# A two-block transformer on one core: contraction groups of 1, 2, 1, 4, 4, 4 tiles over 32 first tiles, squares on two engines, a root on ScalarE, a higher rate of the later modulation

## The chip, the core and the metric

The kernel runs on 1 core of a Trainium2 chip. The metric is the device time of one execution in microseconds. Three runs of the kernel before gave 2420.8, 2422.34 and 2423.11 us; the median is 2422.34. A further execution was recorded by the profiler.

The engines have short names in what follows: TensorE (PE, its weight loads PEld), VectorE (DVE), ScalarE (ACT), GpSimd (POOL) and SyncE (SP, whose queue issues nearly all transfers).

## The reference, cut to what matters

Sequence length 256, model width 2048, batch 1, all in float32. The part that the change touches is the head of the first block:

```python
mod = (c @ w_ada + b_ada)                      # 2048 -> 6 x 2048: shift1, scale1, gate1, ...
h = rmsnorm(x, g_pre_mix) * (1.0 + scale1) + shift1
proj = h @ w_in                                # 2048 -> q_a, k_a, v_a, q_h, f_h, i_h, g_h, gates
...                                            # attention; hgrn2 recurrence; gates; w_out; FFN
```

Behind it come the window attention, the hgrn2 recurrence (two groups of four heads), the gates, the projections, the feed-forward part, and a second block of two layers (attention and gated linear attention). They are the same in both kernels.

## The kernel before

**Tiles and chunks.** Activations lie transposed: 16 tiles of 128 of the 2048 features by 256 positions. A product in float32 is made of three matmuls: activations and weights are split into a high part (`hh`, `wh`) and the rest (`hl`, `wl`), and `mm3` issues wh x hh, wh x hl and wl x hh. Weights come in pieces of 128 x 1024 (512 KB) through a ring of five buffers (`dma_chunks`); SP's transfers use eight semaphores in turn, so that each waits for the landing of the one eight places ahead of it; ScalarE copies the high part (`split_hi`), VectorE subtracts it (`split_lo`), each into a ring of three. One piece feeds 24 matmuls of 256 columns into PSUM tiles `acc`. In this text such a piece with its 24 matmuls is a chunk.

**First stage.** `w_in` has 74 column tiles. The first `G1` = 28 of them are computed group by group along the contraction, since `h` needs the modulation (shift1, scale1), and this needs 2 x 8 MB of `w_ada`, which arrive tile by tile. `KG` says how many of the 16 contraction tiles make a group: 2, 2, 2, 2, 4, 4. In a group of g tiles a chunk holds 8/g column tiles; a group runs over all first tiles (28 x g / 8 chunks), and the partial sums are gathered in SBUF: the first group copies them there on ScalarE, the later groups add them on VectorE, two tiles (512 columns) at a time.

**Modulation pieces.** The first two thirds of the modulation come in 64 pieces of 512 KB (`_mod_flow`, `ada_load`, `ada_use`). `KP` says how many tiles of each group go over TensorE: 4 pieces a tile, as matmuls `ada` that write blocks of 32 columns; four blocks (`nq`) for groups of 2 or more, two for a group of 1. The other tiles (2 each in the last two groups) go over VectorE as a multiply with a sum (`later_piece`, tile `araw`). A list `due` says how many pieces must be used by which chunk; between those points they are spread evenly, three in a burst where possible (`BURST`). Two chunks before a group ends (`LAG`) its successor's columns are transposed (`adat`) and `first_h` is run (`hf` on VectorE, `hh` on ScalarE); at the group's end `first_lo` makes `hl` on VectorE. The first group's pieces are loaded ahead of every weight, and its tiles are the first that TensorE can use. The norm's sum of squares is made by 16 squares on ScalarE and 16 matmuls with a tile of ones (`st`), its root by shifts and three Newton steps on VectorE (`rsqrt`, L541).

**Behind the first stage.** The other tiles of `w_in` are run one by one over the whole contraction (`run`, `win`: two chunks each): the remaining rope tiles, one value tile, 28 gate tiles, 8 tiles `gh`, 4 gate tiles; then `proj` (matmuls `yp`). After each chunk `bg_step` moves background work on: the recurrence `hgrn(0)` and `hgrn(1)` one after the other, the attention `attend1` (four pairs of heads), ropes, and the later modulation (96 multiplies of 512 KB pieces on VectorE, `st_["rate"]` of them per step: `RATES[0]` in this stage, 0.7). A planner (`Clock`, `Timed`) with fixed costs decides when the next step of a background item is put into the program; the engines then execute their instructions in that order. `settle(cond)` puts in background steps without any chunk between them until a condition holds: before gate tile 12 that the first recurrence is done (`0 in ohs`, L1346), before gate tile 20 that the four attentions are, before each tile `gh` that both recurrences are (L1351).

**The recurrence's end** (L1014 to L1055): matmuls `hgx`, a copy on ScalarE (`key`), matmuls `oh`, two copies and a square on ScalarE (`P`, `R`), matmuls `hgq` (sums), twelve small steps on VectorE (`hv`, `hw`, `hr`), transposes `rbk`, a copy (`rc`), four matmuls `hrb`. **The attention's end**: exponentials `s`, scalings of `s`, transposes `atp`, copies `pt`, matmuls `ao`.

Of the kernel before, what the change touches and what calls it, by code (L numbers as in the profile page):

```python
# [7 lines left out]
F32 = mybir.dt.float32  # L8
# [3 lines left out]
AF = mybir.ActivationFunctionType  # L12
ALU = mybir.AluOpType
# [3 lines left out]
D = 2048  # L17
S = 256
META = 16
T2 = S + META  # L20
KT = D // 128
HID = 5632
FGROUPS = [16, 16, 12]
CW = 1024
KG = [2, 2, 2, 2, 4, 4]
KP = [2, 2, 2, 2, 2, 2]
BURST = 3
G1 = 28
GF = 6
G2 = 6  # L30
TF = S + 2
# [37 lines left out]
LIMITS3 = (4.0, 3.5, 1.0)  # L69
LIMITS4 = (4.0, 3.0, 1.0)  # L70
HOP = dict(pe=0.2, dve=0.1, act=0.3)
RATES = (0.7, 0.55, 0.85, 0.2)
FORCE = 2.0


# [9 lines left out]

_FCOLS = {}
_n = 0
for _name, _w in [("ident", 128), ("ones", 128), ("perm1", 128), ("cos2", T2),
                  ("sin2", T2), ("invf", 1), ("esel", 15), ("lo1", 1), ("lo2", 1)]:
    _FCOLS[_name] = (_n, _w)  # L90
    _n += _w
# [4 lines left out]
def _tile_chunks(ap, nk):  # L96
    kc = nk if nk <= 8 else nk // 2
    return [ap[:, k0 * 128:(k0 + kc) * 128] for k0 in range(0, nk, kc)]


def _mod_flow():


    flow, j0 = [], 0
    for g, p in zip(KG, KP):
        pe = [("pe", j0, p, i) for i in range(4 * p)]
# [9 lines left out]
def _plan(a):  # L116

    plan = [a["w_first"][i] for i in range(a["w_first"].shape[0])]
    for i in range(74 - G1):
        plan += _tile_chunks(a["w_in"][i], KT)  # L120
# [99 lines left out]
def body(ctx, tc, a, out, dbg=None):  # L220
# [3 lines left out]
    cst = ctx.enter_context(tc.tile_pool(name="cst", bufs=1))  # L224
# [19 lines left out]
    def bank(name):  # L244
        return ps.tile([128, 512], F32, tag="b", name=name)
# [24 lines left out]
    def t1(name="t1", T=S, dt=F32):  # L270
        return t1p.tile([128, T2], dt, tag="t", name=name)[:, :T]
# [5 lines left out]
    def small(name, n):  # L277
# [3 lines left out]
    TE = Timed(nc.tensor, clock, "pe", lambda n, kw: n / 2400.0 * (  # L281
        4.0 if "lhsT" in kw and kw["lhsT"].dtype == F32 else 1.0) + 0.0025 if n > 16 else 0.11)
    VE = Timed(nc.vector, clock, "dve", lambda n, kw: max(0.07 + n / 960.0, 0.13))
# [3 lines left out]
    tt = VE.tensor_tensor  # L287
    stt = VE.scalar_tensor_tensor
    ts = VE.tensor_scalar
    act = SE.activation  # L290
# [12 lines left out]
    x, xs = [], []  # L303
# [14 lines left out]
    def C(name, i=0, n=None):  # L318
        o, w = _FCOLS[name]
        n = w - i if n is None else n  # L320
        return fc[:, o + i:o + i + n]

    ident = C("ident")
    ones = C("ones")
    identr = cst.tile([128, 128], F32R, name="identr")
    maskr = cst.tile([128, 2 * 128], F32R, name="maskr")
    hh = [cst.tile([128, T2], F32R, name=f"hh{k}") for k in range(KT)]
# [5 lines left out]
    eps1 = cst.tile([128, 1], F32, name="eps1")  # L333
    spare1 = cst.tile([128, 1], F32, name="spare1")
    VE.memset(eps1, 1e-6)


    plan = _plan(a)
# [6 lines left out]
    def dma_chunks(upto):  # L345
        while ptr["dma"] < min(upto, len(plan)):
            i = ptr["dma"]
            n = plan[i].shape[1]
            raws[i] = raw_tile("raw")
            SY.dma_start(out=raws[i][:, :n], in_=plan[i])  # L350
            ptr["dma"] += 1
# [183 lines left out]
    def newton(v, r, t):  # L535

        stt(out=t, in0=r, scalar=-0.5, in1=v, op0=ALU.mult, op1=ALU.mult)
        tt(out=t, in0=t, in1=r, op=ALU.mult)
        stt(out=r, in0=t, scalar=1.5, in1=r, op0=ALU.add, op1=ALU.mult)

    def rsqrt(v, r, t):  # L541

        ts(out=t.bitcast(I32), in0=v.bitcast(I32), scalar1=1, scalar2=None,
           op0=ALU.arith_shift_right)
        ts(out=r.bitcast(I32), in0=t.bitcast(I32), scalar1=-1, scalar2=0x5F3759DF,
           op0=ALU.mult, op1=ALU.add)
        for _ in range(3):
            newton(v, r, t)
# [248 lines left out]
    R = slice(META, T2)  # L797
# [381 lines left out]


    st = bank("st")
    for k in range(KT):
        sq = t1()
        act(out=sq, in_=x[k][:, R], func=AF.Square)
        TE.matmul(st[:, :S], lhsT=ones, rhs=sq, start=(k == 0), stop=(k == KT - 1))
    rbs, v, w = t1("rbs"), t1("rv"), t1("rw")
    ts(out=v, in0=st[:, :S], scalar1=1.0 / D, scalar2=1e-6, op0=ALU.mult, op1=ALU.add)
    rsqrt(v, rbs, w)

    flow = _mod_flow()  # L1190
    ada_todo += [x for f in flow for x in f]
# [7 lines left out]
    def first_lo(k):  # L1199
        stt(out=hl[k][:, :S], in0=hfs.pop(k), scalar=modv(0, k), in1=hh[k][:, :S].bitcast(F32),  # L1200
            op0=ALU.add, op1=ALU.subtract)
# [17 lines left out]
    dma_chunks(4)  # L1219
    for k in range(KG[0]):  # L1220
        first_h(k)
    split_lo(1)
    for k in range(KG[0]):
        first_lo(k)

    ends = [G1 * sum(KG[:i + 1]) // 8 - LAG for i in range(len(KG) - 1)]
    due = [(e, sum(len(f) for f in flow[:i + 2])) for i, e in enumerate(ends)]
    used, want, at, fins = n0, float(n0), 0, []
    k0 = 0
    for gi, g in enumerate(KG):  # L1230
        m = 8 // g
        nch = G1 // m
        last = gi == len(KG) - 1
        for c in range(nch):
            wh, wl = next_chunk()
            banks = []
            if at == 0:

                banks = [bank("acc") for _ in range(m // 2)]
                for w_, h_ in ((wh, hh), (wl, hh), (wh, hl)):  # L1240
                    for i in range(m):
                        for kk in range(g):
                            TE.matmul(banks[i // 2][:, i % 2 * S:(i % 2 + 1) * S],
                                      lhsT=w_[:, (i * g + kk) * 128:(i * g + kk + 1) * 128],
                                      rhs=h_[kk][:, :S],
                                      start=h_ is hh and w_ is wh and kk == 0 and i % 2 == 0,
                                      stop=h_ is hl and kk == g - 1, skip_group_check=True)
# [19 lines left out]
            for i, p in enumerate(banks):  # L1267
                dst, then = first_place(c * m + i * 2)
                p = p.rearrange("p (a t) -> p a t", a=2)
                if gi == 0:  # L1270
                    SE.copy(dst, p)
                else:
                    tt(out=dst, in0=p, in1=dst, op=ALU.add)
                if last:
                    spawn(then, "first")
# [30 lines left out]
        k0 += g  # L1306
    st_["rate"] = RATES[0]
    spawn(hgrn(1), "hg")

    for n in range(G1 - 24, 9):  # L1310
        win(evac_rope1, n)
# [43 lines left out]
    finish("hg", "att", "rope")  # L1355
    st_["rate"] = RATES[1]
    for n in range(KT):
# [106 lines left out]
    finish("pair")  # L1464
    st_["rate"] = RATES[2]
    y, yacc = tiles("y", KT, S), [t1("yacc"), t1("yacc")]
# [65 lines left out]
    for gi, gn in enumerate(FGROUPS):  # L1532
        zz["h"], zz["l"] = tiles("zh", gn, S, F32R), tiles("zl", gn, S, F32R)
        n0 = 0
        if gi == 0:
            next_layer(y, yacc, S, None, S, lambda k: gcol[:, 2, k:k + 1], GF, TF, evac_ff)
            dump("x1", x[5])
            later_sets(5)
            st_["rate"] = RATES[3]
            n0 = GF  # L1540
# [508 lines left out]
    def gla_gate(n, g):  # L2049
# [11 lines left out]
                  v=(evac_gv, False), g=(evac_go, True))  # L2061
# [32 lines left out]
    for k in range(0, KT, 2):  # L2094
# [6 lines left out]
        else:  # L2101
# [3 lines left out]
                          in_=o)  # L2105
# [29 lines left out]
def _layout(inp):  # L2135
    import numpy as np
    f = {k: np.asarray(v) for k, v in inp.items()}
    a = {}
# [6 lines left out]
    for p in sum(_mod_flow(), []):  # L2145
        if p[0] == "pe":
            _, j0, g, i = p
# [4 lines left out]
        else:  # L2152
# [4 lines left out]
    w = f["w_in"][0]  # L2157
# [6 lines left out]
             + g_h + gab[28:])  # L2164
    first = _pack(np, w, order[:G1])
    parts, k0 = [], 0
    for g in KG:
        m = 8 // g
        parts.append(first[:, :, k0 * 128:(k0 + g) * 128].reshape(
            G1 // m, m, 128, g * 128).transpose(0, 2, 1, 3).reshape(G1 // m, 128, CW))  # L2170
        k0 += g
# [13 lines left out]
    start = dict(q=0, k=2048, v=3072, g=4096)  # L2185
# [4 lines left out]
    start = dict(q=(0, 256), k=(1024, 256), v=(2048, 512), g=(4096, 512))  # L2190
# [18 lines left out]
    f32 = np.float32  # L2209
    p = np.arange(128)  # L2210
    perm1 = np.zeros((128, 128), f32)
# [9 lines left out]
    t = np.arange(S)  # L2221
    angs = np.zeros((128, T2), f32)
    for pp in range(128):
# [4 lines left out]
    esel[:, 7] = 1.0  # L2228
    neg = -f32(2.0) ** 126
    sidx, tidx = p[:, None], p[None, :]  # L2230
    fcs = dict(ident=np.eye(128, dtype=f32), ones=np.ones((128, 128), f32), perm1=perm1,
               cos2=np.cos(angs.astype(np.float64)).astype(f32),
               sin2=(np.sin(angs.astype(np.float64)) * turn).astype(f32),
               invf=invf, esel=esel, lo1=np.where(p % 64 // 16 == 1, f32(-1), f32(0))[:, None],
# [30 lines left out]
```

## Time and profile before

| what | kernel before |
|---|---|
| median of 3 runs | 2422.34 us |
| the profiled execution | 2425.35 us |
| its span, first to last instruction | 2423.4 us |
| TensorE busy | 2391.2 us, 99% |
| VectorE busy | 1724.0 us, 71% |
| ScalarE busy | 1195.8 us, 49% |
| read from HBM | 492.68 MB, 204 GB/s over the span |
| mean granted TensorE clock | 0.994 |

The profiled execution is 3.0 us longer than the median, and 2 us of it lie outside the span. Busy time on TensorE is pipelined time: an engine that shows 10.00 of 10 us may still run its matmuls at the lower clock, so the granted clock of a stretch stands beside it. An idle engine costs time where the last-ending chain goes through it; here that is TensorE for 94% of the span.

### The profile page before, as it was taken

What the parts mean: (1) busy time and instruction counts of PE and PEld (TensorE: products, weight loads), DVE (VectorE), ACT (ScalarE), POOL (GpSimd) and SP (SyncE); (2) the same over time, 40 slices, a digit from 0 to 9 for tenths busy, and PEclk for the clock granted to TensorE, in tenths of its full rate; (3) what the DMA queues carried; (4) which work ended last, traced back from release to release, by engine and by line L of the source; (5) the groups of instructions that cost most, each with busy time, mean ns of one, the idle gap of its engine ahead of it and who ended that gap; (6) DMA issues with size and microseconds to landing.
All of it is one profiled execution on the core that took longest, in us unless ns stands there. A gap on an engine that the chain in (4) does not pass through costs nothing.

```text
span 2423.4 us, 49168 instructions
## 1 busy us (share of the span) xinstructions
PE 2391.2 (99%) x20217; PEld 2349.9 (97%) x20217; DVE 1724.0 (71%) x2986; ACT 1195.8 (49%) x1923; POOL 63.3 (3%) x128
## 2 busy tenths in 40 slices
PE   8999999999999999999999999999999999999998
PEld 7999999999999999999999999999999999999997
DVE  4897978888867775577755666777777466788664
ACT  4335565444445444444434444545555456855443
POOL 0000000000000000000000000121110000000000
PEclk9999999999999999999999999999999999999999
DMA  9975768798885666666665556554443545444453
GB/s 400 364 288 171 235 201 267 247 307 295 305 291 161 210 223 223 221 218 220 225 211 186 184 170 170 173 162 140 151 145 118 174 149 173 160 137 147 158 183 113
DMA packets 144273, 501.33 MB, mean 207 GB/s; under 512 B 17088, under 2 KB 19904, under 8 KB 144048
## 3 DMA queue, kind: packets, MB, share of 16 engines
q1 hardware_dynamic: 139840, 493.15, 60.6%
q0 software_dynamic: 3072, 3.35, 0.4%
q8 instruction: 158, 2.59, 0.4%
q10 hardware_dynamic: 1136, 1.68, 0.2%
q14 instruction: 67, 0.55, 0.1%
HBM read 492.68 MB, written 2.10 MB: 204 GB/s over the span
## 4 chain that ended last, share of the span: by engine, by line
PE 94%; DMA 3%; DVE 2%; ACT 1%; issue 0%; SPq 0%; DVEq 0%; ACTq 0%
PE acc L214 76%; PE wave L214 5%; PE yp L214 4%; PE hgs L214 1%; DMA araw<-in_w_adat 1%; PE sc L214 1%; DVE wl L214 1%; PE go L214 1%; PE st L214 1%; PE ada L214 1%; PE o L214 1%; DMA araw<-in_w_mod 1%; DMA raw<-in_w_out 1%; PE tp L214 0%; DVE araw L214 0%
## 5 line engine op out<-in xcount | busy, mean ns | idle before, releaser
L214 ACT CAST wh<-raw 128x1024 fp32r<-128x1024 f32 (+1 forms) x754 | 774.2, 1027 | 1100.8 <-PE acc L214 710.2
L214 PE MATMUL acc<-hh,wh 128*128 128x256 f32 (+2 forms) x4112 | 1182.3, 288 | 2.5 <-ACT hh L214 2.5
L214 PE MATMUL acc<-hl,wh 128*128 128x256 f32 (+2 forms) x4112 | 1165.2, 284 | 3.7 <-DVE hl L214 3.7
L214 PE MATMUL acc<-hh,wl 128*128 128x256 f32 (+2 forms) x4112 | 1166.3, 284 | 2.3 <-DVE wl L214 2.3
L214 DVE TENSOR_TENSOR wl<-raw,wh 128x1024 fp32r<-128x1024 f32 (+1 forms) x754 | 900.1, 1194 | 369.5 <-ACT wh L214 365.8
L214 PEld LDWEIGHTS acc<-hh,wh 128*128 128x128 f32 x4112 | 778.5, 189 | 10.9 <-issue 5.2
L214 PEld LDWEIGHTS acc<-hl,wh 128*128 128x128 f32 x4112 | 778.2, 189 | 5.3 <-DVE hl L214 4.3
L214 PEld LDWEIGHTS acc<-hh,wl 128*128 128x128 f32 x4112 | 778.4, 190 | 3.3 <-DVE wl L214 3.1
L214 PE MATMUL acc<-zl,wh 128*128 128x256 f32 x704 | 198.2, 282 | 0.0
L214 PE MATMUL acc<-zh,wl 128*128 128x256 f32 x704 | 198.0, 281 | 0.0
L214 PE MATMUL acc<-zh,wh 128*128 128x256 f32 x704 | 197.0, 280 | 0.0
L214 DVE SCALAR_TENSOR_TENSOR araw<-araw,cb 128x1024 f32<-128x1024 f32 x144 | 175.6, 1219 | 13.5 <-DMA araw<-in_w_adat 13.4
L214 PEld LDWEIGHTS acc<-zh,wl 128*128 128x128 f32 x704 | 133.3, 189 | 0.0
L214 PEld LDWEIGHTS acc<-zh,wh 128*128 128x128 f32 x704 | 133.1, 189 | 0.0
L214 PEld LDWEIGHTS acc<-zl,wh 128*128 128x128 f32 x704 | 132.2, 188 | 0.0
L214 PE MATMUL wave<-hl,wh 128*128 128x272 f32 (+1 forms) x288 | 82.1, 294 | 0.8 <-DVE hl L214 0.8
L214 PE MATMUL wave<-hh,wh 128*128 128x272 f32 (+1 forms) x288 | 81.3, 291 | 0.1
L214 PE MATMUL wave<-hh,wl 128*128 128x272 f32 (+1 forms) x288 | 80.1, 287 | 0.0
L214 PE MATMUL acc<-oph,wh 128*128 128x272 f32 x256 | 74.2, 290 | 0.0
L214 PE MATMUL acc<-oph,wl 128*128 128x272 f32 x256 | 74.1, 289 | 0.0
L214 PE MATMUL acc<-opl,wh 128*128 128x272 f32 x256 | 73.7, 288 | 0.0
L214 PE MATMUL acc<-gpl,wh 128*128 128x256 f32 x256 | 72.1, 282 | 0.0
(373 smaller groups left out, 2845.8 us busy)
## 6 DMA issues: line engine op xcount, KB each, us to landing
raw<-in_w_ffn_in SPq DMA_DIRECT2D x164, 512.0 KB, 4.3
araw<-in_w_adat SPq DMA_DIRECT2D x128, 512.0 KB, 4.7
raw<-in_w_in SPq DMA_DIRECT2D x92, 512.0 KB, 4.9
raw<-in_gla_w_in SPq DMA_DIRECT2D x86, 512.0 KB, 3.5
raw<-in_attn_w_in SPq DMA_DIRECT2D x84, 512.0 KB, 3.6
araw<-in_w_mod SPq DMA_DIRECT2D x64, 512.0 KB, 8.6
raw<-in_w_ffn_out SPq DMA_DIRECT2D x64, 512.0 KB, 4.4
raw<-in_w_first SPq DMA_DIRECT2D x56, 512.0 KB, 6.5
```

Of the source, the lines that this page charges most:

```text
L214: return f(*args, **kw)
```

## The change

`KG` becomes 1, 2, 1, 4, 4, 4 and `KP` 1, 2, 1, 4, 4, 2, so that 56 pieces go over TensorE and 8 over VectorE, and `G1` becomes 32: the first stage has 4 + 8 + 4 + 16 + 16 + 16 = 64 chunks, and one rope tile is left for `win` instead of five. The square sums are made for four tiles at once, half on ScalarE and half on VectorE, added, and summed by 8 matmuls; the root is ScalarE's with one Newton step. In the first group VectorE makes every other copy. `RATES[0]` is 0.76. The tile of ones is set by a memset and no longer loaded.

```diff
-KG = [2, 2, 2, 2, 4, 4]
-KP = [2, 2, 2, 2, 2, 2]
+KG = [1, 2, 1, 4, 4, 4]
+KP = [1, 2, 1, 4, 4, 2]
-G1 = 28
+G1 = 32
-RATES = (0.7, 0.55, 0.85, 0.2)
+RATES = (0.76, 0.55, 0.85, 0.2)
...
-    ones = C("ones")
+    ones = cst.tile([128, 128], F32, name="ones")
...
+    VE.memset(ones, 1.0)
...
     st = bank("st")
-    for k in range(KT):
-        sq = t1()
-        act(out=sq, in_=x[k][:, R], func=AF.Square)
-        TE.matmul(st[:, :S], lhsT=ones, rhs=sq, start=(k == 0), stop=(k == KT - 1))
+    act(out=spare1, in_=eps1, func=AF.Sqrt)
+    for g in range(4):
+        v4 = xs[g].rearrange("p (a t) -> p a t", a=4)[:, :, R]
+        sa, sb = t2("sa"), t2("sb")
+        act(out=sa, in_=v4[:, 0:2], func=AF.Square)
+        tt(out=sb, in0=v4[:, 2:4], in1=v4[:, 2:4], op=ALU.mult)
+        tt(out=sa, in0=sa, in1=sb, op=ALU.add)
+        for i in range(2):
+            TE.matmul(st[:, :S], lhsT=ones, rhs=sa[:, i], start=(g == 0 and i == 0),
+                      stop=(g == 3 and i == 1))
     rbs, v, w = t1("rbs"), t1("rv"), t1("rw")
+    act(out=rbs, in_=st[:, :S], func=AF.Sqrt, scale=1.0 / D, bias=eps1)
     ts(out=v, in0=st[:, :S], scalar1=1.0 / D, scalar2=1e-6, op0=ALU.mult, op1=ALU.add)
-    rsqrt(v, rbs, w)
+    VE.reciprocal(out=rbs, in_=rbs)
+    newton(v, rbs, w)
...
-                if gi == 0:
+                if gi == 0 and i % 2:
+                    VE.tensor_copy(dst, p)
+                elif gi == 0:
                     SE.copy(dst, p)
```

**Where instructions stand.** SP's queue at the start, from the last tile of `x` on (`araw` are modulation pieces, `raw` weight chunks); before:

```order
L214 DMA x_95<-in_xt 128x1088
L214 DMA araw_213<-in_w_mod 128x1024
L214 DMA araw_215<-in_w_mod 128x1024
L214 DMA araw_217<-in_w_mod 128x1024
L214 DMA araw_219<-in_w_mod 128x1024
L214 DMA araw_221<-in_w_mod 128x1024
L214 DMA araw_223<-in_w_mod 128x1024
L214 DMA araw_225<-in_w_mod 128x1024
L214 DMA araw_227<-in_w_mod 128x1024
L214 DMA raw_229<-in_w_first 128x1024
L214 DMA raw_231<-in_w_first 128x1024
L214 DMA araw_274<-in_w_mod 128x1024
```

and now:

```order
L214 DMA x_95<-in_xt 128x1088
L214 DMA araw_190<-in_w_mod 128x1024
L214 DMA araw_192<-in_w_mod 128x1024
L214 DMA araw_194<-in_w_mod 128x1024
L214 DMA araw_196<-in_w_mod 128x1024
L214 DMA raw_198<-in_w_first 128x1024
L214 DMA raw_200<-in_w_first 128x1024
L214 DMA araw_227<-in_w_mod 128x1024
L214 DMA raw_229<-in_w_first 128x1024
L214 DMA araw_239<-in_w_mod 128x1024
L214 DMA araw_249<-in_w_mod 128x1024
L214 DMA araw_251<-in_w_mod 128x1024
```

Four modulation pieces fewer stand ahead of the first weight chunk; the ninth to the twelfth transfer are now two weights, a piece and a weight.

TensorE at the end of the first recurrence, before, around the transposes `rbk`; a chunk of `acc` matmuls stands ahead of them and another behind:

```order
L214 MATMUL acc_4210<-hh14_113,wl_4185 128x256
L214 MATMUL acc_4210<-hh15_114,wh_4133 128x256
L214 MATMUL acc_4210<-hl15_130,wh_4133 128x256
L214 MATMUL acc_4210<-hh15_114,wl_4185 128x256
L214 MATMUL rbk_4334<-fc_85,hr_4251 4x128 x2
L214 MATMUL acc_4349<-hh0_99,wh_4187 128x256
L214 MATMUL acc_4349<-hl0_115,wh_4187 128x256
L214 MATMUL acc_4349<-hh0_99,wl_4235 128x256
```

Now, behind chunk 92 (before gate tile 12), from the last `oh` on:

```order
L214 MATMUL oh_4463<-key_2849,vtok0_2689 128x128
L214 MATMUL oh_4463<-S0_2850,vtok0_2689 128x128
L214 MATMUL hgq_4484<-ones_97,R_4471 128x1 x8
L214 MATMUL atp_4508<-fc_85,s_4364 128x128 x2
L214 MATMUL atp_4513<-fc_85,s_4367 128x128 x2
L214 MATMUL rbk_4520<-fc_85,hr_4494 4x128 x2
L214 MATMUL atp_4524<-fc_85,s_4370 128x128 x4
L214 MATMUL atp_4531<-fc_85,s_4373 128x128 x4
L214 MATMUL hrb_4538<-rc_4518,fc_85 128x256
L214 MATMUL ao_4541<-pt_4511,akv_150 64x128
```

Ahead of these rows stand, behind the chunk, `atp` x8, `hgx` x4, `ao` x12 and the other `oh`; behind them the rest of `ao` and three more `hrb`, and only then chunk 93. Between the steps of the recurrence's end there were chunks before, and there is attention or nothing now.

TensorE at the end of the second recurrence, before, around `hgq`:

```order
L214 MATMUL acc_5790<-hl7_122,wh_5688 128x256
L214 MATMUL acc_5790<-hh7_106,wl_5726 128x256
L214 MATMUL hgq_5821<-fc_85,R_5788 128x1 x8
L214 MATMUL acc_5790<-hh8_107,wh_5728 128x256
L214 MATMUL acc_5790<-hl8_123,wh_5728 128x256
L214 MATMUL acc_5790<-hh8_107,wl_5765 128x256
```

and now, behind chunk 124 (before the first tile `gh`):

```order
L214 MATMUL oh_5822<-S0_4603,vtok1_2840 128x128
L214 MATMUL hgq_5832<-ones_97,R_5830 128x1 x8
L214 MATMUL rbk_5858<-fc_85,hr_5842 4x128 x2
L214 MATMUL hrb_5862<-rc_5856,fc_85 128x256
L214 MATMUL hrb_5865<-rc_5856,fc_85 128x256
L214 MATMUL hrb_5868<-rc_5856,fc_85 128x256
L214 MATMUL hrb_5871<-rc_5856,fc_85 128x256
L214 MATMUL acc_5874<-hh0_100,wh_5724 128x256
L214 MATMUL acc_5874<-hl0_116,wh_5724 128x256
```

Ahead of these rows stand `hgx` x4 and `oh`, directly behind the chunk. Before, a chunk stood between `hgx` and `oh`, `oh` and `hgq`, `hgq` and `rbk`, `rbk` and `hrb`, and between the first `hrb` and the other three; now none does. From the first `yp` on the order on TensorE is the same in both kernels.

## Rows read from the trace of the kernel before

**Rows 1.** The page, busy time of each engine: us, share of span, instructions.

```profile
PE 2391.2 (99%) x20217; PEld 2349.9 (97%) x20217; DVE 1724.0 (71%) x2986; ACT 1195.8 (49%) x1923; POOL 63.3 (3%) x128
```

**Rows 2.** Waits of TensorE: tile, releaser; us in total, times, longest.

```profile
PE st L214 <- ACT t L214: 8.0, 1, 8.0
...
PE acc L214 <- DVE hl L214: 3.7, 2, 3.5
...
PE acc L214 <- ACT hh L214: 2.5, 1, 2.5
```

**Rows 3.** Stretches: length, each engine's busy us (instructions), PEclk, DMA share, GB/s.

```profile
20.00:30.00 10.00, 7.11 (x78) 6.53 (x70) 7.34 (x16) 4.10 (x6) 0.00 (x0) 0.68 1.02 417
30.00:40.00 10.00, 10.00 (x119) 9.67 (x119) 4.72 (x4) 5.96 (x9) 0.00 (x0) 0.98 1.03 419
...
130.00:140.00 10.00, 9.72 (x95) 9.50 (x95) 7.95 (x17) 2.39 (x4) 0.00 (x0) 0.69 1.01 394
```

**Rows 4.** Timeline of the start: start us, length, engine, operation, tiles, count, idle before.

```profile
17.72 3.70 PE L214 MATMUL ada<-araw,vec 128*32 128x128 f32 x128
...
23.11 0.15 DVE L214 TENSOR_TENSOR mod<-adat,vec 128x4 f32<-128x4 f32 x1
```

**Rows 5.** Chain that ended last, first stage: start us, length, engine and tile, count.

```profile
24.65 8.60 PE acc L214 x48
33.25 1.45 PE ada L214 x48
34.70 5.85 PE acc L214 x48
...
52.48 1.01 PE ada L214 x32
```

**Rows 6.** Timeline of SP's queue, one issue.

```profile
34.95 0.33 SPq L214 DMA_DIRECT2D raw<-in_w_first  x1
```

**Rows 7.** Timeline of VectorE around the transition to the first four-tile group.

```profile
124.68 1.67 DVE L214 SCALAR_TENSOR_TENSOR hf<-x,gcol,rbs 128x256 f32<-128x256 f32 x4
126.27 1.22 DVE L214 TENSOR_TENSOR wl<-raw,wh 128x1024 fp32r<-128x1024 f32 x1
127.41 1.28 DVE L214 TENSOR_TENSOR ih<-acc,ih 128x512 f32<-128x512 f32 x2
...
129.75 1.67 DVE L214 SCALAR_TENSOR_TENSOR hl<-hf,mod,hh 128x256 fp32r<-128x256 f32 x4
```

**Rows 8.** Timeline of TensorE, end of the second recurrence.

```profile
459.19 1.05 PE L214 MATMUL hgx<-R 128*128 128x128 f32 x8
...
462.89 0.38 PE L214 MATMUL oh<-S,vtok 128*128 128x128 f32 x2
...
465.35 0.39 PE L214 MATMUL oh<-S,vtok 128*128 128x128 f32 x2
...
468.38 1.84 PE L214 MATMUL hgq<-fc,R 128*128 128x1 f32 x16
...
479.27 1.46 PE L214 MATMUL hrb<-rc,fc 128*128 128x256 f32 x6
```

**Rows 9.** Timeline of ScalarE at the same place.

```profile
460.28 0.59 ACT L214 COPY key<-hgx 128x512 f32<-128x512 f32 x1
...
466.40 1.06 ACT L214 ACTIVATE R<-P 128x1024 f32<-128x1024 f32 x1
```

**Rows 10.** Timeline of VectorE there: first and last of twelve small steps.

```profile
470.26 0.17 DVE L214 TENSOR_SCALAR hv<-hgq 128x8 f32<-128x8 f32 x1 [4.94 <-PE hgq L214]
...
472.49 0.17 DVE L214 SCALAR_TENSOR_TENSOR hr<-hw,hr 128x8 f32<-128x8 f32 x1
```

**Rows 11.** Timeline of ScalarE: first and last of eight exponentials; eight scalings.

```profile
321.07 0.36 ACT L214 ACTIVATE s<-asc,mx 128x128 f32<-128x128 f32 x1
...
324.15 0.25 ACT L214 ACTIVATION_READ_ACCUMULATOR s<-asc,mx 128x1 f32 x1
...
345.23 2.88 ACT L214 ACTIVATE s<-s,mx 128x128 f32<-128x128 f32 x8
```

More of the change, by code (lines that the diff above doesn't have):

```diff
@@ L87 @@
 _n = 0
-for _name, _w in [("ident", 128), ("ones", 128), ("perm1", 128), ("cos2", T2),
+for _name, _w in [("ident", 128), ("perm1", 128), ("cos2", T2),
                   ("sin2", T2), ("invf", 1), ("esel", 15), ("lo1", 1), ("lo2", 1)]:
@@ L2230, in _layout @@
     sidx, tidx = p[:, None], p[None, :]
-    fcs = dict(ident=np.eye(128, dtype=f32), ones=np.ones((128, 128), f32), perm1=perm1,
+    fcs = dict(ident=np.eye(128, dtype=f32), perm1=perm1,
                cos2=np.cos(angs.astype(np.float64)).astype(f32),
```

## The prediction

> **What bounds the kernel now.** First the busy shares on the page: TensorE is busy for 99% of the span [rows 1], so only three things can move the time: idle stretches of TensorE, stretches at its lower clock, and matmuls added or dropped. Then the waits of TensorE: the long ones that the change can touch lie in the first stage, 8.0 us at the very start, 2.5 us before the first acc matmul and 3.7 us for hl, 3.5 of them in one wait [rows 2]. Third, the table by stretches of ten microseconds: after both of the later waits the granted clock averages 0.68 and 0.69 of 2.4 GHz, part of the stretch standing at 1.2 GHz, and until 40 us and beyond the DMA engines are full, share 1.03 at 419 GB/s [rows 3]. So at the start the DMA queue is a second bound, right behind TensorE. The other entries of that list name tiles of later layers. An engine takes its instructions in the order of the program; a background step that stands between two chunks of acc matmuls is therefore harmless, and several in one heap, with no acc matmul between them, are not.
>
> I count in chunks of 24 acc matmuls (one weight tile of 512 KB). Two chunks take 5.85 us, a burst of three modulation pieces 1.45, one of two 1.01 [rows 5]: 2.92 a chunk, and 0.44 a piece plus 0.13 a burst.
>
> **The start: earlier first matmul, but the queue decides.** The first group needs 4 modulation pieces instead of 8. In the trace the pieces' matmuls end at 21.4, VectorE adds the bias at 23.11 [rows 4] and the first acc matmul runs at 24.65 [rows 5]; about 0.6 of these 3.2 is VectorE still at its long root. The fourth piece is eighth in SP's queue, 15 transfers of 1.25 us (512 KB at 419 GB/s [rows 3]) before the one that lands at 34.9 (below), so it lands at 15 to 16: the wait for it sets the start, and halving the statistics' matmuls, the squares on two engines and the root on ScalarE is worth nothing by itself; its cover is that transfer, and if that were gone it would be worth at most the 8.0 us wait. Piece 4 done at about 16, plus the chain of copy, transpose, column, hf and hh of 2.6, gives a first acc matmul at 18.6, 6.0 earlier.
>
> It does not stay. The planner now wants 12 pieces by the second chunk and, bursts being three long, the program puts pieces 5 to 13 on TensorE ahead of chunk 3. Piece 13 is the 23rd transfer of SP's queue. Before, the transfer at that place frees the issue of the one eight places later, at 34.95 [rows 6]; all of them have the same size in both kernels, so piece 13 lands at 34.9. One transfer's time sooner or later (33.7, 36.1) is possible; I take the row. TensorE has then used 2 chunks and has mostly waited since about 28 us, with short bursts, so I take its clock to be at 1.2 GHz, as after the 2.5 and 3.5 us waits: then about 2.9 us are lost until it rises (5.7 us at half speed, as from 24.65 to 30.4, since the stretch from 30 on has 0.98 [rows 3, 5]). Chunk 5 starts at 34.9 + 0.88 (piece 13) + 2 x 2.92 + 2.9 + 1.9 (pieces 14 and 15) = 46.4. Before it starts at 34.70 + 5.85 + 1.45 = 42.0 [rows 5]. **Term 1: +4.4** (bounds +0.3, with the landing at 33.7 and the full clock, and +5.6, with that at 36.1).
>
> **Pieces.** 56 pieces now go over TensorE instead of 48. From chunk 5 on there were 34 left in 8 bursts of three and 5 of two, 16.6 us; now there are 41 in 15 bursts. A piece of a one-tile group writes two blocks of 32 columns in place of four. The rows show that blocks overlap: 48 ada matmuls take 1.45, 0.030 each, while 8 hgx matmuls with as many streamed columns but all 128 weight columns take 1.05, 0.13 each [rows 5, 8]. With half the blocks I take twice the time, 0.88 a piece (bounds 0.44 and 1.9). 41 x 0.44 + 0.44 + 15 x 0.13 = 20.4. **Term 2: +3.8** (3.3 to 5). The Trainium skill, "TensorEngine Tiling (Array Packing)", section "Performance Considerations", says that a stationary operand of 32 columns can be run four at a time; the ratio of the rows, about four, agrees, and by it a piece that offers two blocks gets half the gain, 0.88 by its estimate too, which speaks against one-tile groups.
>
> **The transition that stalls.** The 3.5 us wait for hl [rows 2] comes from VectorE: four hf (1.67), a weight split (1.22), two adds (1.28), a modulation multiply and four hl (1.67) stand in one row [rows 7], behind 8 modulation multiplies before it. The changed kernel gives the first four-tile group no VectorE pieces, but the one-tile group ahead of it has eight tiles a chunk, so four adds (2.4) and a split (1.14) a chunk, 3.5 against 2.9 of TensorE. With the transpose of the columns at chunk 15, hf follows, then split, four adds and hl: 0.4 + 1.7 + 1.1 + 2.4 + 0.4 = 6.0 after it, against 5.2 until chunk 17 needs the first hl, and the next three come 0.4 apart: about 1.1 us of waiting (0 to 4, the upper end with a lower clock). Gone are 3.5 + 3.1 (the share 0.69 of ten microseconds [rows 3]) and 0.2 of short waits. **Term 3: -5.7** (-6.8 to -2.8). ScalarE's and VectorE's shared copies of the first group lie beside the wait for piece 13 and cost nothing. The rate of 0.76 over 84 steps gives as many later pieces as 0.70 over 92: nothing.
>
> **What moves: the recurrence's end.** 32 first tiles leave four tiles fewer in the stage behind. But the stage still insists on the first recurrence before gate tile 12 and on the second before the hg gates. Counted from the recurrence's start, 8 chunks fewer lie ahead of the first point. In the changed order chunk 92 is followed by hgx, ao, oh, hgq, atp, rbk, atp, hrb, ao, hrb with no acc matmul among them, and chunk 124 by hgx, oh, hgq, rbk, hrb. Before, each of these had a chunk of 2.9 us behind it, under which the other engines did their part.
>
> Priced at chunk 124, from the same steps at 459 us: hgx 1.05; ScalarE's copy 0.59 until oh may go on; oh 2.85; then copy and square until 1.72 after the last oh [rows 8, 9]; hgq 1.84; twelve VectorE steps, 2.40 [rows 10]; transpose 0.4, copy 0.45, four hrb 1.9. TensorE waits 0.65 + 1.75 + 2.45 + 0.45. **Term 4: +5.3** (4.5 to 5.5). At chunk 92 the last two attention groups stand in the heap. ScalarE carries, from the end of chunk 90, s x8 (2.9), eight exponentials (3.3) [rows 11], three R steps and copies, two weight casts: about 12.2 us until ao has its operand, against 9.5 of TensorE's work: a wait of 2.7. Then 1.7 for the square, 2.15 for the twelve steps (0.3 covered by atp) and 0.3 for the last copies. **Term 5: +6.8** (5 to 8.3).
>
> Each heap holds 2.5 us of idle in 3 us, much like the stretches behind which the clock stood at 1.2 GHz [rows 2, 3]. A lower clock costs about 3.1 there; no row shows a heap of this kind. **Term 6: +5**, between 0 and 9 (three falls), nearer to two falls of which one lies partly in a wait.
>
> Sum: 4.4 + 3.8 - 5.7 + 5.3 + 6.8 + 5 = +19.6. From the first yp matmul on the order of TensorE is unchanged, and it is busy throughout, so the shift is carried to the end. The profiled execution took 2425.35, so its like is 2445.0; the median before is 2422.34, and the same shift gives **2442**.
>
> **Rivals.** *The heaps cost nothing* (0.13): TensorE would go on with acc matmuls behind a waiting one, or the other engines would be done early. Then terms 4 to 6 go, +2.5, 2425: no difference that counts. It decides at the square behind oh, where ScalarE has 1.7 us of work that cannot start before. Against it: while TensorE waited 3.5 us for hl, the hh matmul of the same tile that needs no hl waited too. The Trainium skill, "TensorE: Matmul & The Clock Gate", section "The mechanism", has matmuls start and end strictly in program order; the trace agrees, and by that rule the heaps cost their waits.
> *The start is kept* (0.08, and 0.07 with the first): piece 13 does not hold chunk 3, because the queue is quicker than before or the wait smaller. Then chunk 5 starts at 18.6 + 4 x 2.92 + 11 pieces (6.7) = 37.0, term 1 is -5.0, the sum +10, 2432. Only with the first rival on top, -7, 2415, is the kernel faster.
> *The one-tile group chokes on VectorE* (0.1): the 0.6 us that it lacks a chunk add up over four chunks with no slack from before, 3.5 us and a lower clock of 3, so +5 more, 2447.
>
> **How the numbers follow.** Chances: the forecast, start lost and heaps waiting, 0.62; heaps free 0.13; start kept 0.08; both 0.07; the one-tile group choking 0.10. The range of the forecast: with no fall of the clock (-5), the start at its lower end (-4.1) and the heaps at theirs (-2.6) it is 2430; with three falls (+4), the later landing (+1.2) and the transition at its upper end (+2.9) it is 2450. The second and third rival lie inside; what is left out is the first, alone or with the second, 0.20. A measurement of this kernel tells some 0.2%, 4.8 us, from no change. Slower by more: 0.62 + 0.08 + 0.10 = 0.80; within: 0.13; faster: 0.07.
>
> **What would show it.** First acc matmul near 18.6, but chunk 3 at 35 to 37 behind a landing piece, at half clock; TensorE waiting for DVE hl once, about 1 us, near 92; no 3.5 us wait; waits of TensorE for ScalarE and VectorE at hgq, rbk, ao and oh, near 350 and 480, of some 12 us together, with a granted clock under 1 beside them. The prediction is wrong if TensorE shows no waits there, or if chunk 5 starts before 42.

## The result and the profile after

The changed kernel takes 2451.24 us (median of 4 runs, 2449.84 to 2453.62) against 2422.73 for the kernel before in the same measurement: 1.0127 times as long, 95% interval 1.0115 to 1.0139, slower by 28.5 us. The forecast was 2442, at most 2450: the direction was right, the size too small. The profiled execution took 2451.48 us, its span is 2449.6, 26.2 more than that of before; the other 2.3 us lie in the profiled execution of before, which was 2.6 us above its own median.

The page's first part, busy time of each engine (us, share of the span, instructions), as [rows 1]:

```profile
PE 2406.8 (98%) x20075; PEld 2353.9 (96%) x20075; DVE 1730.0 (71%) x2984; ACT 1191.6 (49%) x1904; POOL 63.0 (3%) x128
```

TensorE is still the bound, with fewer matmuls and more time: it is the stretches in which it stands or runs at the lower clock that grew. The waits of TensorE (tile, releaser; us in total, times, longest), as [rows 2]:

```profile
PE st L214 <- DVE sa L214: 6.3, 1, 6.3
...
PE rbk L214 <- DVE hr L214: 4.1, 2, 2.5
PE hgq L214 <- ACT R L214: 3.5, 2, 1.8
PE ada L214 <- DMA araw<-in_w_mod: 3.4, 5, 1.8
PE acc L214 <- DVE hl L214: 3.2, 3, 1.8
...
PE ao L214 <- ACT pt L214: 1.7, 1, 1.7
...
PE oh L214 <- ACT key L214: 0.7, 1, 0.7
PE hrb L214 <- ACT rc L214: 0.5, 1, 0.5
```

The waits for rbk, hgq, ao, oh and hrb, 10.5 us together, are new: before, TensorE shows no wait at all from 340 to 500 us. The wait for hl, 3.7 in [rows 2], is still 3.2, split in three.

The stretches (length, busy us of each engine, PEclk, DMA share, GB/s), as [rows 3], with those of the two heaps:

```profile
20.00:30.00 10.00, 9.22 (x132) 8.23 (x135) 5.77 (x7) 4.63 (x7) 0.00 (x0) 0.90 1.02 417
30.00:40.00 10.00, 7.33 (x82) 5.95 (x75) 1.99 (x5) 1.28 (x4) 0.00 (x0) 0.66 1.03 418
...
140.00:150.00 10.00, 8.15 (x63) 7.95 (x62) 9.79 (x22) 5.97 (x11) 0.00 (x0) 0.92 0.55 195
150.00:160.00 10.00, 10.00 (x114) 9.67 (x113) 5.92 (x7) 2.69 (x3) 0.00 (x0) 0.91 0.99 375
...
360.00:370.00 10.00, 8.25 (x66) 7.33 (x65) 3.94 (x9) 6.87 (x25) 0.00 (x0) 0.84 0.49 166
370.00:380.00 10.00, 6.62 (x37) 5.97 (x37) 2.00 (x12) 5.86 (x14) 0.00 (x0) 0.67 0.00 0
380.00:390.00 10.00, 10.00 (x75) 9.03 (x74) 5.18 (x12) 3.12 (x6) 0.00 (x0) 0.81 0.08 23
...
490.00:500.00 10.00, 6.74 (x57) 6.27 (x55) 3.19 (x9) 4.05 (x6) 0.00 (x0) 1.00 0.52 186
500.00:510.00 10.00, 7.85 (x40) 6.64 (x41) 5.30 (x15) 0.93 (x2) 0.00 (x0) 0.66 0.08 22
```

Where before had two stretches with a low clock in the first 500 us [rows 3], now there are four places: the start, 148, the first heap and the second. The first heap in TensorE's timeline (start, length, tiles, count, idle before it), as [rows 8]:

```profile
365.31 1.94 PE L214 MATMUL ao<-pt,akv 128*64 128x128 f32 x20 [1.70 <-ACT pt L214]
...
373.34 3.32 PE L214 MATMUL hgq<-ones,R 128*128 128x1 f32 x16 [1.77 <-ACT R L214]
376.52 1.09 PE L214 MATMUL atp<-fc,s 128*128 128x128 f32 x4
379.22 0.58 PE L214 MATMUL rbk<-fc,hr 128*4 128x128 f32 x2 [1.61 <-DVE hr L214]
```

16 hgq matmuls take 3.32 here and 1.84 in [rows 8]: they ran at 1.2 GHz. From the last acc matmul ahead of the heap to the first behind it, 361.2 to 385.7, it is 24.5 us: 5.1 of them are these three waits, and for 13.7 the clock stood at half.

In sum, by matching places in the two traces: at the first yp matmul, the end of all that the change moves, the changed kernel is 26.0 us behind (574.7 against 548.7), and from there to the end the two take the same time. Of the 26.0, 3.8 are the start, 3.6 the pieces, the acc matmuls with their stalls give back 2.4, and the two heaps cost 21. The 21 can be checked in one stretch: from the end of the first stage to the first yp matmul it takes 325.6 us, where before, with eight chunks of 2.92 us more in it, takes 328.4, so it grew by 20.6. In the four other traces with both heaps that stretch takes 322.8 to 324.6, so 21 is the upper end; the start's 3.8, too, is of this one pair (below, term 1). (From here a chunk is numbered by how many are done when it begins, except chunks 3 and 5, the third and the fifth, as in the prediction.)

### The profile page after: what moved, and what is told of

It reads as the page before. It is cut to its first block, busy times and chain, and to the rows that moved or that the text cites. A ratio compares the mean times of both kernels' runs of the same rounds, so it can differ in the third digit from the quotient of the medians.

```text
span 2449.6 us, 48865 instructions
## 1 busy us (share of the span) xinstructions
PE 2406.8 (98%) x20075; PEld 2353.9 (96%) x20075; DVE 1730.0 (71%) x2984; ACT 1191.6 (49%) x1904; POOL 63.0 (3%) x128
## 4 chain that ended last, share of the span: by engine, by line
PE 90%; DVE 5%; DMA 4%; ACT 1%; issue 1%; DVEq 0%; ACTq 0%
PE acc L214 73%; PE wave L214 4%; PE yp L214 3%; DMA araw<-in_w_adat 2%; DVE wl L214 1%; DMA araw<-in_w_mod 1%; PE hgs L214 1%; DVE araw L214 1%; PE ada L214 1%; PE sc L214 1%; PE go L214 1%; PE o L214 1%; DMA raw<-in_w_out 1%; PE tp L214 0%; PE asc L214 0%
## 5 line engine op out<-in xcount | busy, mean ns | idle before, releaser
L214 DVE SCALAR_TENSOR_TENSOR araw<-araw,cb 128x1024 f32<-128x1024 f32 x136 | 165.8, 1219 | 18.4 <-DMA araw<-in_w_adat 18.1
```

What stands on the lines that cost most here:

```text
L214: return f(*args, **kw)
```

## The experiments

Ratios are to the kernel before, in runs on the same chip.

| kernel | median us | ratio | 95% interval |
|---|---|---|---|
| the change | 2451.24 | 1.0127 | 1.0115 to 1.0139 |
| before, rate 0.76 | 2430.46 | 1.0049 | 1.0033 to 1.0066 |
| before, 32 tiles | 2438.42 | 1.0065 | 1.0050 to 1.0080 |
| before, 32 tiles and 0.76 | 2445.29 | 1.0098 | 1.0081 to 1.0115 |
| change, rate 0.70 | 2441.86 | 1.0082 | 1.0067 to 1.0097 |
| change, 0.70 then 0.72 | 2435.85 | 1.0064 | 1.0048 to 1.0079 |
| change, heaps filled | 2445.53 | 1.0099 | 1.0084 to 1.0114 |
| change, angles later | 2451.62 | 1.0122 | 1.0105 to 1.0139 |
| change, groups 2, 2, 4, 4, 4 | 2445.27 | 1.0099 | 1.0084 to 1.0114 |
| change, bursts of four | 2446.80 | one run | |
| before, squares and root | 2423.64 | 1.0009 | 1.0000 to 1.0019 |
| before, KP[4] = 4 | 2420.03 | 0.9993 | 0.9984 to 1.0002 |
| before, groups 2, 2, 4, 4, 4 | 2421.07 | 0.9997 | 0.9988 to 1.0006 |

**What makes the heaps: tiles or rate?** The forecast blamed the four tiles moved into the first stage and called the rate worth nothing. Four kernels take the two apart. The changed kernel with the old rate:

```diff
-RATES = (0.76, 0.55, 0.85, 0.2)
+RATES = (0.7, 0.55, 0.85, 0.2)
```

> The changed kernel with the later modulation's rate back at 0.70. In its order the heap at chunk 124 is gone (hgx, oh, hgq, rbk and hrb have a chunk between them) and at chunk 92 only hgq, one ao, rbk and hrb stand together. Theory, that the two heaps cost 21 us and that the rate makes them: of the waits at oh, hgq, rbk and ao some 1.5 to 2.5 us are left, and no lower clock near 370 and 500: 18 to 20 us less than the changed kernel, 2431 to 2434. Rival, that the four tiles moved into the first stage make the heaps, as the prediction had it, and the rate does nothing: 2451.

The kernel before with 32 tiles alone:

```diff
-G1 = 28
+G1 = 32
```

> The kernel before with G1 = 32 alone (groups 2, 2, 2, 2, 4, 4, rate 0.70). Rival, the prediction's terms 4 to 6 as they stand (the moved tiles make the heaps): 17 to 21 us slower, 2440 to 2444. Theory, that it takes the rate too: only the small heap at chunk 92 (hgq, ao, rbk, hrb), 0 to 3 us, 2422 to 2426.

The kernel before with both:

```diff
-G1 = 28
+G1 = 32
-RATES = (0.7, 0.55, 0.85, 0.2)
+RATES = (0.76, 0.55, 0.85, 0.2)
```

> The kernel before with G1 = 32 and the rate at 0.76, start and groups as before. Its order has both heaps, row for row those of the changed kernel. If the heaps are worth 21 us whatever stands ahead of them: 2443 to 2445. If the changed start and the one-tile groups are the larger part and the heaps give their idle time back later: under 2432.

The kernel before with the rate alone:

```diff
-RATES = (0.7, 0.55, 0.85, 0.2)
+RATES = (0.76, 0.55, 0.85, 0.2)
```

> The kernel before with the rate at 0.76 alone: 28 first tiles, groups and start as before. Its order has the heap at chunk 124 (hgx, oh, hgq, rbk and four hrb with no acc matmul between) and none of weight at chunk 92. Theory, that the rate makes that heap and that it costs its waits and a fall of the clock: 5.5 us of waits at oh, hgq, rbk and hrb and 2.4 of lower clock near 490, so 7 to 9 us slower, 2428 to 2431. Rival, the prediction's own (the rate is worth nothing, only the moved tiles make heaps): 2420 to 2423.

The rate alone makes the second heap, in the kernel before, and it costs 10.3 us by the medians (7 to 9 were expected; in the traces the stretch from the end of the first stage to the first yp matmul grows by 9.0). Waits of TensorE from 440 to 500 us in that kernel:

```profile
PE rbk L214 <- DVE hr L214: 2.5, 1, 2.5
PE hgq L214 <- ACT R L214: 1.8, 1, 1.8
PE oh L214 <- ACT key L214: 0.7, 1, 0.7
PE hrb L214 <- ACT rc L214: 0.5, 1, 0.5
```

The same four waits as in the changed kernel, to a tenth, with 28 tiles. The tiles alone leave only a small heap at chunk 92, 1.6 us of waits there (rbk 1.1, hrb 0.5) and 3.4 us at the first yp matmul. With both, both heaps are there, and 2445.29 lies at the upper end of what was expected; the first heap needs the tiles and the rate together. In the changed kernel the old rate takes 17.3 us out of the stretch from the end of the first 64 chunks to the first yp matmul (308.2 against 325.6), leaving waits of 1.6 from 340 to 520. Why the rate does it is read from the order of the instructions and from the planner's code, and no run tests it by itself: each later piece is a VectorE step of 1.22 us, and a background step is put behind a chunk only while VectorE's and ScalarE's planned times are near TensorE's. With more chunks that carry a piece, four chunks stand between two steps of the second recurrence (`hgs`) from chunk 105 on, where three did, it falls behind, and what is left of it must be done at once where a tile `gh` needs it.

But neither gain arrives in full: 2441.86 for the change at rate 0.70, where 2431 to 2434 was expected. The rate of 0.70 loses 6.5 us again later, 32 tiles alone 9.6: from the first yp matmul to the first matmul into a tile `wave`, with which the feed-forward part begins, it takes 196.3 and 199.5 us, where before, the change and 32 tiles with 0.76 take 190. In the kernel with rate 0.70, TensorE at the place, and VectorE ahead of it:

```profile
730.48 0.39 PE L214 MATMUL acc<-hh,wl 128*128 128x256 f32 x1 [3.75 <-DVE wl L214]
```

```profile
727.80 1.23 DVE L214 SCALAR_TENSOR_TENSOR araw<-araw,cb 128x1024 f32<-128x1024 f32 x1 [1.64 <-DMA araw<-in_w_adat]
...
729.20 3.49 DVE L214 TENSOR_TENSOR wl<-raw,wh 128x1024 fp32r<-128x1024 f32 x3
```

and its stretches:

```profile
720.00:730.00 10.00, 5.96 (x48) 5.55 (x47) 5.99 (x10) 3.65 (x5) 0.00 (x0) 1.00 0.90 340
730.00:740.00 10.00, 9.52 (x67) 9.52 (x68) 6.58 (x14) 5.02 (x23) 0.00 (x0) 0.83 0.71 226
```

The program finishes the set of later pieces ahead of a fixed output tile. Ahead of the first yp matmul VectorE has done 63 later pieces before, 61 in the change and 56 with 32 tiles and 0.70; so 21 pieces instead of 16 stand between the projection and that tile, and the last of them wait for their own transfers while the weight split behind them waits too. Sparing that wait is what the higher rate bought. Both theories for 32 tiles alone (0 to 3, and 17 to 21) missed it: 16.5 came, 9.6 of it in this stretch.

**The rate, split.** The missing pieces can be done in the projection instead; in the changed kernel:

```diff
-RATES = (0.76, 0.55, 0.85, 0.2)
+RATES = (0.7, 0.72, 0.85, 0.2)
```

> The changed kernel with the rate at 0.70 up to the projection, as in the last run but two, and 0.72 instead of 0.55 in the projection's 32 steps (some 5 pieces more there). Theory, that the run with 0.70 gave back 6.5 us between the first yp matmul and the first wave matmul because pieces that were left over stood in a row on VectorE at 705 to 730, and TensorE waited 4.0 us for wl behind them: that wait and the lower clock after it go, the stretch from yp to wave is again 190 us, and the time is that of the changed kernel less the 17.6 us of the heaps, 2433 to 2436. Rival, that VectorE has no room in the projection either: 2440 to 2443, with as much waiting for wl at other places.

By the median the theory's number: 15.4 us less than the change, by the ratios 15.2. Of the four runs three lie at 2435 to 2437 and one at 2440.62. It is this one whose trace there is, and in it the stretch from yp to wave is 197.0 us, with waits for wl at 654, 695 and 718: there the rival shows, although only 17 pieces were left behind the projection. So the number of left-over pieces is not the whole cause of the late waits; how the three shorter runs spent that stretch no trace tells.

**What the clock costs in the heaps.** Matmuls into a bank that nobody reads, only where TensorE waited:

```diff
         act(out=sq, in_=o_, func=AF.Square)
+        keep_warm(14)
...
         r = rstd_tokens(ss, 4, S)
+        keep_warm(18)
         yield 1.0
```

and likewise 4 behind hgx and 14 ahead of ao.

> The changed kernel with matmuls whose result nobody reads put on TensorE inside both heaps, about as many as the waits there are long (4 behind hgx, 14 ahead of ao in the first heap, 14 ahead of hgq, 18 ahead of rbk). They add work only where TensorE waited. Theory, that the idle time lets the clock fall: the stretches at half clock at 367 to 384 and 500 to 507 go, 8 to 10 us less, 2441 to 2443. Rival, that the clock falls because the heap's own matmuls load TensorE little (transposes, narrow operands): no gain, or up to 3 us more, 2451 to 2454.

The stretches of that kernel:

```profile
360.00:370.00 10.00, 10.00 (x97) 9.62 (x96) 3.53 (x9) 7.46 (x25) 0.00 (x0) 1.00 0.46 162
370.00:380.00 10.00, 9.88 (x89) 8.98 (x88) 2.62 (x14) 6.64 (x17) 0.00 (x0) 1.00 0.00 0
380.00:390.00 10.00, 10.00 (x84) 9.92 (x84) 9.05 (x18) 4.79 (x6) 0.00 (x0) 1.00 0.50 151
490.00:500.00 10.00, 9.17 (x68) 8.26 (x67) 4.13 (x17) 2.02 (x3) 0.00 (x0) 1.00 0.12 48
500.00:510.00 10.00, 10.00 (x87) 10.00 (x86) 8.53 (x13) 3.44 (x4) 0.00 (x0) 1.00 0.74 222
```

The clock is 1.00 throughout, and the heap's own matmuls (transposes, one-column sums) run at it: the theory holds, the rival falls. The gain from the end of the first stage to the first yp matmul is 7.0 us (6.8 for the whole by the ratios), a little under the 8 to 10, since the 86 filling matmuls took 11.8 us in place of 9.6 us of waits. The clock alone is thus worth 7.0 + 2.2 = 9.2 us of the heaps, against the trace of the change, in which the clock stood at half for 20.5 us in the two; where it stood at half for 13.7, as in three of the four other traces with both heaps, it can be worth no more than half of that, 6.9.

**The wait for hl at 147.6.** The forecast had one wait of 1.1 us near 92, at an edge (where one group of contraction tiles ends and the next begins); there is one of 0.7 there, one of 0.7 at 200 and one of 1.8 at 147.6, at the edge between two four-tile groups. VectorE ahead of it in the changed kernel:

```profile
140.18 1.33 DVE L214 SCALAR_TENSOR_TENSOR ang<-trn,ang 128x256 f32<-128x256 f32 x3
141.55 0.29 DVE L214 TENSOR_SCALAR ang<-ang 128x256 f32<-128x256 f32 x1
...
142.61 1.67 DVE L214 SCALAR_TENSOR_TENSOR hf<-x,gcol,rbs 128x256 f32<-128x256 f32 x4
...
145.94 1.21 DVE L214 SCALAR_TENSOR_TENSOR araw<-araw,cb 128x1024 f32<-128x1024 f32 x1
...
147.08 1.67 DVE L214 SCALAR_TENSOR_TENSOR hl<-hf,mod,hh 128x256 fp32r<-128x256 f32 x4
```

```diff
-C1 = 21
+C1 = 34
```

> The changed kernel with the constants and angles of the later stage spawned at chunk 34 instead of 21. Theory, that the 2.0 us wait for hl at 147.6 comes from the five angle operations (2.6 us of VectorE) which chunk 32, the edge between the two last four-tile groups, now shares with them: the wait and the half clock behind it (1.7 us) go, 3 to 4 us less, 2447 to 2448, with a first hl before 146. Rival, that the group's own VectorE work (four hf, two adds, a split, a modulation piece, four hl) makes it: the wait stays, 2451.

In the kernel with the angles later, the row of hl on VectorE, TensorE's waits for hl from 130 to 210 us, and the stretches about the two edges:

```profile
145.54 1.67 DVE L214 SCALAR_TENSOR_TENSOR hl<-hf,mod,hh 128x256 fp32r<-128x256 f32 x4
```

```profile
PE acc L214 <- DVE hl L214: 3.5, 2, 2.4
```

```profile
140.00:150.00 10.00, 8.93 (x75) 8.73 (x74) 9.26 (x18) 4.62 (x7) 0.00 (x0) 1.00 0.74 272
150.00:160.00 10.00, 10.00 (x121) 9.67 (x121) 7.19 (x11) 3.00 (x4) 0.12 (x1) 1.00 0.96 352
190.00:200.00 10.00, 7.47 (x61) 7.07 (x59) 9.72 (x23) 6.74 (x10) 0.00 (x0) 1.00 0.38 125
200.00:210.00 10.00, 10.00 (x87) 10.00 (x86) 8.55 (x10) 4.15 (x4) 0.00 (x0) 1.00 0.70 219
```

With the angles gone from there hl starts at 145.54, 1.54 us sooner, the wait is 1.1, the clock stays at 1.00 from 140 to 160, and chunk 48 begins 2.7 us sooner, 0.8 of which was there before the edge. The wait that remains is put down to the group's own work, so each theory has a part. And the time is unchanged: the angles now stand at 189.6 to 191.7, ahead of the next edge, where TensorE waits 2.4 for hl instead of 0.7, and 2.8 us more are lost in the output stage behind waits for wl. Work that was moved off one edge went to another.

**The start.** First the changed kernel with longer bursts:

```diff
-BURST = 3
+BURST = 4
```

> The changed kernel with bursts of up to four pieces. Ahead of chunk 3 then stand 12 pieces and not 13. If the landing of the last of them sets when chunk 3 begins (34.8 us for piece 13, one transfer of 1.25 us each): piece 12 lands at 33.5 and chunk 3 begins 1.7 us sooner (1.25 and the matmuls of one piece), near 35.0. If something else holds it (the clock, VectorE's adds): 36.7 as before. The time of the whole: 0 to 3 us less.

The last piece ahead of chunk 3, in the change and with bursts of four:

```profile
34.83 1.92 PE L214 MATMUL ada<-araw,vec 128*32 128x128 f32 x16 [0.24 <-DMA araw<-in_w_mod]
```

```profile
32.41 0.64 PE L214 MATMUL ada<-araw,vec 128*32 128x128 f32 x16 [0.60 <-DMA araw<-in_w_mod]
```

One piece fewer, and chunk 3 begins at 32.98 instead of 36.68: the landing of the last piece holds it. The gain is 3.7, not 1.7, for two reasons. A weight, too, moved behind the last piece, so that this is the 21st transfer and no longer the 23rd, and its matmuls start 2.4 us sooner (32.41 against 34.83). And the clock keeps 1.00 there, where the change has 0.66 from 30 to 40 us: from the last piece's start to chunk 3 it takes 0.57 and not 1.85, the other 1.3. After 64 chunks it is 4.1 us ahead, and the one run took 2446.80, 4.4 less than the change's median and 25.5 more than the kernel before in the same measurement, where the change has 28.5.

Then the changed kernel without its one-tile groups:

```diff
-KG = [1, 2, 1, 4, 4, 4]
-KP = [1, 2, 1, 4, 4, 2]
+KG = [2, 2, 4, 4, 4]
+KP = [2, 2, 4, 4, 2]
```

> The changed kernel with contraction groups 2, 2, 4, 4, 4 (TensorE's pieces 2, 2, 4, 4, 2), all else as in it: no one-tile group, and the start of the kernel before. By the terms: first acc matmul near 24, term 1 (3.8 measured) and the 0.9 for the pieces of half width go, so 4 to 5 us less, 2446 to 2447. If the earlier start were worth its 6 us it would be slower, 2454 to 2457. If VectorE stalls at the edge from two tiles to four at chunk 16, as in the kernel before, it stays at 2450 to 2452.

6.0 us less by the medians, 6.8 by the ratios, more than the 4 to 5 expected: first acc matmul at 23.98, 64 chunks done at 241.9 instead of 249.1. The lead is 10.0 at the first yp matmul, but 3.4 of it are lost again before the first wave matmul, behind waits for wl. So the groups 1, 2, 1, which start TensorE 5.3 us earlier, cost what they gain and more. Of the lead, some 2.7 lie behind the first stage, where the same heaps cost this trace less: the clock stood at half for 13.7 us and not for 20.5.

The third is the change's start step alone: in the kernel before, the loop of 16 squares and the root on VectorE give way to the new statistics.

```diff
-    for k in range(KT):
-        sq = t1()
-        act(out=sq, in_=x[k][:, R], func=AF.Square)
...
+    for g in range(4):
...
+        act(out=sa, in_=v4[:, 0:2], func=AF.Square)
+        tt(out=sb, in0=v4[:, 2:4], in1=v4[:, 2:4], op=ALU.mult)
+        tt(out=sa, in0=sa, in1=sb, op=ALU.add)
```

> The kernel before with the squares and the root of the change alone: pair sums on two engines, 8 instead of 16 matmuls into st, root by ScalarE. By the prediction the wait for the pieces sets the start and this is worth nothing by itself, at most the 0.6 us that VectorE's long root holds the columns: first acc matmul at 23.9 to 24.7, 2421 to 2423. Rival, that the statistics set the start: the 1.7 us by which st begins earlier arrive at the end, 2420 or less.

First acc matmul at 24.05 instead of 24.65, and nothing gained at the end: by the medians it is 2.8 us slower, with an interval that begins at 1.0000. The 0.6 is not shown to be the edit's: in two more traces whose start is that of before, instruction for instruction (before with rate 0.76, and with KP[4] = 4), the first acc matmul runs at 23.39 and 23.42.

**Is there a version that beats both?** Two candidates, on the kernel before.

```diff
-KP = [2, 2, 2, 2, 2, 2]
+KP = [2, 2, 2, 2, 4, 2]
```

> The kernel before with KP[4] = 4 alone: all 16 modulation pieces of the first four-tile group go over TensorE, none over VectorE ahead of the edge at chunk 28. By the prediction's term 3 the wait of 3.5 us for hl and the half clock behind it (3.1) go, and 8 pieces more cost 3.9: 2419 to 2420. Rival, from the changed kernel's 2.0 us wait at its edge between four-tile groups: four hf, two adds, a split and four hl alone keep a wait of 1 to 2 us and the lower clock, nothing is gained, 2421 to 2424.

The wait for hl falls from 3.7 to 0.9, and the stretch at half clock from 129 to 136 us is gone. (The second need not come from the edit: before with rate 0.76, whose first stage is that of before, still waits 2.6 us there and shows 1.00 from 120 to 140.) The median is 1.3 us lower; the interval, 0.9984 to 1.0002, holds the forecast gain of 2 to 3 us and no gain at all.

```diff
-KG = [2, 2, 2, 2, 4, 4]
-KP = [2, 2, 2, 2, 2, 2]
-C1 = 21
+KG = [2, 2, 4, 4, 4]
+KP = [2, 2, 4, 4, 2]
+C1 = 15
```

and the squares and root of the change.

> The kernel before with groups 2, 2, 4, 4, 4 over its 28 first tiles (TensorE's pieces 2, 2, 4, 4, 2), the squares and root of the change, the rate at 0.70, and the constants spawned at chunk 15, so that the angles lie between two edges. No heap in its order (hgx, oh, hgq, rbk and hrb stand a chunk apart, as before). If heaps and rate make the loss of the changed kernel and the groups are harmless: no long wait for hl (-6.8), 8 pieces more (+3.9), columns 0.6 earlier, 2417 to 2420. Rival, that fewer and larger groups cost by themselves (VectorE stalls at each four-tile edge): 2424 to 2430.

2421.07, neither theory's number: this kernel as a whole costs nothing and gains nothing. What its parts (larger groups, eight pieces more, the statistics, earlier angles) cost or gain singly is not shown. No kernel here beats the one before by more than the measurement tells.

## Why the prediction was right and wrong

- **The places and the kind of the loss were right, one cause and two sizes were wrong.** At the first yp matmul the shift is 26.0 where 19.6 was forecast: term 3 gave back 3.3 less and the clock of term 6 cost 5.5 more, while the other four terms came out 2.4 lower together. Another 2.5 of the 9.2 us by which the forecast fell short are the profiled executions, before's lying above its median and the change's on it, and 0.3 the median of before, 2422.73 in this measurement.
- **Term 1, the start: right.** First acc matmul 18.70 (18.6 forecast), chunk 3 at 36.68 behind the landing of piece 13 and at half clock, chunk 5 at 45.69 (46.4): +3.8 for +4.4. The bursts of four show the landing to be the cause. The size holds less well: the five traces with the change's start begin chunk 5 at 44.84 to 45.69, the three with that of before at 39.81 to 41.92, so the start costs 2.9 to 5.9, and the trace of before is the latest of its three. The 18.6 was partly luck: TensorE's row `ada` runs from 12.87 to 16.56 directly behind the sums of squares, with no wait for any piece, so its own work and not the fourth piece's landing set the start, and the chain behind it took 2.1 and not 2.6.
- **Term 2, the pieces: right.** +3.6 for +3.8.
- **Term 3, the transition: too good.** -2.4 for -5.7 in this pair of traces. The step that failed is "about 1.1 us of waiting": it looked at the edge near 92 only. The edge between the four-tile groups moved to 147, where the angles, a later piece, four hf and four hl meet on VectorE: 1.8 us of waiting and 1.7 lost at half clock. The 3.1 of half clock that was to go is not in every execution of before either: in the trace with rate 0.76, of the same first stage, it is missing, and the first stage ends 4.4 us sooner.
- **Terms 4 and 5, the waits in the heaps: right in size, wrong in cause.** 5.4 for 5.3 and 5.1 for 6.8; they were priced from the new order, and that needs no cause. The step that failed is "8 chunks fewer lie ahead of the first point", and with it "the rate of 0.76 over 84 steps gives as many later pieces as 0.70 over 92: nothing". The count held (61 and 63 pieces). But the price of a rate is not the number of its pieces: it is what the planner puts off behind them. The tiles alone cost 3.4 there, the rate alone the whole second heap.
- **Term 6, the clock: half of what it was.** The heaps cost 21, their waits 10.5; the filled kernel puts the clock at 9.2 against 5, and 1.3 are left unexplained. The step that failed is "nearer to two falls of which one lies partly in a wait": there were three, and in the first heap alone it stood at half for 13.7 us. The range's three falls of 3.1 would have come near it.
- **The rivals.** That the heaps cost nothing fell by their waits, and that the start is kept by chunk 5 at 45.69. The one-tile group did not choke: its only wait for hl, near 92, was 0.7.

## What to carry to other kernels

Where a planner fits background work between matmuls, a higher rate is not free merely because the total of its pieces is unchanged: look in the new order for what it pushes back, and price that at the point where the delayed chain is due. The heaps of small dependent matmuls cost their waits, 10.5 us here, and in one trace almost as much again in the clock, 9.2; filling the waits with matmuls gave that second part back, less what the filling took. A step moved off one edge goes to another: look at every edge of the new arrangement, not only at the one that stalled.

## What the runs showed of the hardware

The clock did not fall by the length of a wait alone. The 1.8 us wait at 147.6 was followed by half clock (0.92 and 0.91 from 140 to 160), the wait of 2.4 us at 199 with the angles moved was not (1.00 from 190 to 210). At the edge to the first four-tile group a wait of 2.7 us was followed by half clock in the kernel before with the new squares and root (0.69 from 130 to 140), one of 2.6 us in that with rate 0.76 was not (1.00). And the same heap, with the same order, stood at half clock for 13.7 us in the trace of the change, for 10.2 with bursts of four and for 6.8 with the angles moved. Single traces place a fall of the clock within some microseconds only.
